# Shifts of the modulated norms: added per row tile with the eviction of plain transposes, in place of PSUM products with a selector and the identity

## The chip, the cores and the metric

The kernel runs on one core of one Trainium2 chip. The metric is device time in microseconds of one execution. Engines are named as the profile names them: PE (TensorE), ACT (ScalarE), DVE (VectorE), POOL (GpSimd), SP (SyncE, which issues the loads).

## The reference

Two blocks work on x [256, 1024] one after the other, all in float32. The first block (two layers) uses plain RMS norms. The second block modulates its norms by vectors made from a condition:

```python
def modulate(h, shift, scale):
    return h * (1 + scale[:, None, :]) + shift[:, None, :]

def macaron_ffn(x, mod3, norm_pre, norm_post, w_gate, w_up, w_down):
    h = modulate(rms_norm_2(x, norm_pre), mod3[:, 0], mod3[:, 1])
    y = (jax.nn.silu(h @ w_gate) * (h @ w_up)) @ w_down
    return x + MACARON_WEIGHT * mod3[:, 2][:, None, :] * rms_norm_2(y, norm_post)
...
        x = macaron_ffn(x, mod[:, 0:3], *ffn1)
        ctx = macaron_ffn(ctx, mod_ctx[:, 0:3], *ffn1)
...
            h_ctx_f, h_ctx_b = context_states(ctx, mod_ctx[:, 3:6], mix_norm_pre[layer], w_in[layer],
...
        x, _, _ = mix_sublayer(x, mod[:, 3:6], h_ctx_f, h_ctx_b, *mix)
        x = macaron_ffn(x, mod[:, 6:9], *ffn2)
```

`ctx` is a second sequence of 256 tokens. So the second block norms x three times and ctx twice with a scale and a shift per column, and each result is the input of a product with weights.

## The kernel before, in words

Tokens stand on the partitions in tiles of 128 (x has two, the context two). Products need the normed input the other way round, with the 1024 columns on partitions: eight row tiles of 128 columns by 128 tokens. Since float32 products are slow, every operand is held as two float32r parts whose sum is exact, a high part `hi` and a low part `lo`; a product is then three products. Weights are loaded by SP into one of three `raw` buffers, ACT writes their high part (L505) and DVE the low part (L506). The products are L519 (weights stationary, `mm_feat`) and L527 (activations stationary, `mm_tok`).

A norm (`pre_norm`, L545) works on one token tile: ACT squares it (L535), POOL makes the reciprocal root (L540, L542), and for each half of 512 columns DVE multiplies with that and with a gain row (L554, tile `xn`), PE turns the half into one bank of PSUM (tile `tp`, two buffers), and `split_to` takes it out: ACT writes `hi` (L510), then DVE writes `lo = tp - hi` (L511), each in one instruction of 128 x 512. Without a shift PE's part is four transposes (L559). With a shift, each of the four row tiles is a block of two products into one place of PSUM: the shift, held as 16 rows (two exact parts of eight row tiles), times a column of a selector (L561, float32r), and `xn` times the identity added to it (L563, float32, which runs as two passes, so two records each). `mod_gain` (L1171) makes the gain row and these 16 shift rows: ACT L1179, DVE L1181 and L1182, a transpose L1184, ACT L1186.

The norms with a shift are ten token tiles, that is 20 halves or 80 blocks, in four stages: the context's first norm (`context_norm`, L1049, beside the last products of the first block), x's first norm (`to_both`, L1059, between the first products for the context and the same products for x), the four tiles at the end of the joint feed-forward part (`ffn_both`, L1257 to L1267, with the gate and residual L1260 and L1264 before each norm, and units of the modulation, `ada`, L1131 to L1140, between), and the norm before the last feed-forward part (`boundary`, L1080). The boundaries of the first block have the same steps with plain transposes.

The order of the work on each engine is not the program's. `Order` (L207) collects all instructions, gives each a cost, and runs a list schedule: a step goes to the engine that can start first, and of the instructions that it could start then, to the first in the program. Tiles of one tag (`xn` has four, `tp` two, `raw` three) are handed out in program order. The result is pinned, so each engine runs its instructions in that order and a waiting one holds up all behind it. Its dependencies hold a bank of PSUM as one whole, and two accesses of it depend on each other even if both read:

```python
            whole = self.tags[t][0] == 'psum'
            for c, d, mm, k, kw in seen.get(t, ()):
                if (w or kw or whole) and c < b and a < d and m & mm:
                    need.add(k)
```

`finish` in `mix2` (L1553) already takes transposes out per row tile with a scalar per partition: ACT L1576 for `hi`, DVE L1577 for `lo`, each 128 x 128.

Of the kernel before, what the change touches and what calls it, by code (L numbers as in the profile page):

```python
# [10 lines left out]
FT = mybir.dt.float32  # L11
# [7 lines left out]
T = 256  # L19
# [13 lines left out]
def _tiles(w):  # L33
    """[1024, 128 n] -> [128, n, 8 * 128]: per output tile, the row tiles side by side."""
    n = w.shape[1] // 128
    return w.reshape(8, 128, n, 128).transpose(1, 2, 0, 3).reshape(128, n, 1024)
# [8 lines left out]
def _rows(w, n):  # L45
    """[128 k, c] -> [k / n, 128, n c]: n row tiles side by side."""
# [5 lines left out]
def _block_diag(w):  # L52
    """[4, 64, 64] -> [128, 2, 128]"""
# [7 lines left out]
def _ffn_up(a, b):  # L61
    """two [1024, 2816] -> [22, 128, 2048]"""
# [11 lines left out]
def shape_constants():  # L74
# [15 lines left out]
    # means over windows less the token itself: columns of tokens 0..143 from tokens 0..127, the rest from 128..255  # L90
# [113 lines left out]
# the units of the modulation that VectorE computes  # L204
# [3 lines left out]
class Order:  # L208
    """The order in which every engine issues the traced instructions: a list schedule with the engines' costs
    (Tile's own estimates are far off for float32 products and for GpSimd), pinned by issue-only edges.  # L210
    A step goes to the engine that can start first; among the instructions that it could start then, the one
    that comes first in the program goes."""
# [7 lines left out]
    # the clock of the tensor engine halves after a window that it was idle in for long  # L220
# [10 lines left out]
    # ---- what an instruction touches: (tile, partitions, columns as a bit mask); a bank of PSUM is one whole  # L231
# [19 lines left out]
    def graph(self):  # L251
        """dependencies: for each instruction the earlier ones it has to wait for"""
# [23 lines left out]
    # ---- costs  # L276
    def cost(self, i, e):
        """how long an instruction holds its engine; on the tensor engine also how long it streams"""
# [25 lines left out]
    # ---- the schedule  # L304
    def prepare(self):
# [8 lines left out]
        # activations of one table stay together  # L314
# [10 lines left out]
    def schedule(self, phases):  # L325
# [6 lines left out]
        # tiles: those of a tag are allocated in program order; a pool's once the pool before is done  # L332
# [103 lines left out]
class Pool:  # L436
    """a tile pool whose tiles the order knows"""
# [9 lines left out]
class Core:  # L447
# [33 lines left out]
    def outputs(self):  # L481
        """accumulators of a [256, 1024] product: per token tile, two banks of 512 columns"""
        self.o = [[self.acc_tile() for _ in range(2)] for _ in range(2)]
# [1190 lines left out]
```

## Time and profile before

| | us |
|---|---|
| runs shown, median (lowest to highest) | 1512.03 (1502.82 to 1514.5) |
| span of the profiled execution | 1506.0 |
| PE busy | 1466.4 |
| DVE busy | 905.6 |
| ACT busy | 683.5 |
| POOL busy | 78.5 |

The span runs from the first to the last instruction of the profiled execution, and the page gives no other time of it: 1506.0 lies inside the spread of the runs, 6.0 under their median. Busy PE includes time in which its matmuls are pipelined. In the rows below "A:B" is a stretch in us from the span's start, "x4" the number of instructions that a row merges, and "[1.20 <-DVE xn L554]" says that the engine sat idle for 1.20 us just before and what ended it. PEclk is the granted clock of PE as a share of 2.4 GHz.

### The profile page before, as it was taken

The page shows a single profiled execution, that of the slowest core. Times are in us where ns is not written, and L with a number is a line of the kernel's source. Part 1 is how long each engine was busy: PE and PEld are TensorE (multiplying, and loading weights), DVE is VectorE, ACT ScalarE, POOL GpSimd, SP SyncE. Part 2 cuts the span into 40 slices and gives each one's busy share as a digit, 9 for nine tenths or more (in the row PEclk, how much of TensorE's full clock was granted, in tenths as well). Part 3 has the DMA queues.
Part 4 walks back from the last instruction along what each step waited for, and adds up shares of the span by engine and source line. Part 5 has one row for each costly group of instructions (what it writes and reads, how often), then busy time and mean ns, then how long its engine had stood idle before and what let it go on. Part 6 is the DMA issues. An engine that isn't in the chain of part 4 may idle for free.

```text
span 1506.0 us, 21907 instructions
## 1 busy us (share of the span) xinstructions
PE 1466.4 (97%) x8857; PEld 1262.4 (84%) x8857; DVE 905.6 (60%) x1487; ACT 683.5 (45%) x1180; POOL 78.5 (5%) x146
## 2 busy tenths in 40 slices
PE   8999999999999999999999999999999998899998
PEld 7966999998877999988888888888697776699997
DVE  5667777777777777763774532454566536455554
ACT  5335655555345555552422222443544464454443
POOL 1002000002001000000000000000200212100000
PEclk8889999999789999998999999999999999799999
DMA  6407645546416554522555442232352033145552
GB/s 249 171 36 286 238 168 196 196 162 244 165 57 248 186 194 170 196 84 81 202 193 212 179 140 84 73 110 98 139 183 80 28 135 118 57 168 179 203 179 82
DMA packets 35833, 232.30 MB, mean 154 GB/s; under 512 B 4242, under 2 KB 5394, under 8 KB 10004
## 3 DMA queue, kind: packets, MB, share of 16 engines
q1 hardware_dynamic: 35732, 230.91, 42.6%
q8 instruction: 69, 1.13, 0.3%
q14 instruction: 32, 0.26, 0.0%
HBM read 229.85 MB, written 1.05 MB: 153 GB/s over the span
## 4 chain that ended last, share of the span: by engine, by line
PE 89%; DVE 3%; DMA 3%; ACT 2%; issue 1%; POOL 1%; SPq 0%; DVEq 0%; POOLq 0%; ACTq 0%
PE mm L519 39%; PE acc L527 25%; PE acc L519 11%; PE tp L563 3%; PE tp L561 1%; PE mm L839 1%; DVE wl L506 1%; PE mm L1131 1%; PE tp L856 1%; DMA raw<-in_fu_dram 1%; ACT wh L505 1%; PE tp L1167 1%; PE tp L711 1%; DMA raw<-in_wo_dram 0%; PE acc L1512 0%
## 5 line engine op out<-in xcount | busy, mean ns | idle before, releaser
L506 DVE TENSOR_TENSOR wl<-raw,wh 128x1024 fp32r<-128x1024 f32 (+2 forms) x345 | 414.0, 1209 | 281.9 <-ACT wh L505 270.3
L505 ACT ACTIVATE wh<-raw 128x1024 fp32r<-128x1024 f32 (+2 forms) x345 | 356.5, 1046 | 346.0 <-PE mm L519 178.1
L519 PE MATMUL mm<-hh,wh 128*128 128x256 f32 (+1 forms) x1440 | 228.0, 301 | 1.2 <-DVE ex L994 1.2
L519 PE MATMUL mm<-hl,wh 128*128 128x256 f32 (+1 forms) x1440 | 227.4, 298 | 0.0
L519 PE MATMUL mm<-hh,wl 128*128 128x256 f32 (+1 forms) x1440 | 223.0, 297 | 0.0
L519 PEld LDWEIGHTS mm<-hh,wh 128*128 128x128 f32 x1440 | 202.7, 195 | 11.6 <-ACT ex L992 1.4
L519 PEld LDWEIGHTS mm<-hl,wh 128*128 128x128 f32 x1440 | 202.0, 193 | 9.4
L519 PEld LDWEIGHTS mm<-hh,wl 128*128 128x128 f32 x1440 | 197.4, 193 | 6.6
L527 PE MATMUL acc<-wh,hl 128*128 128x512 f32 (+1 forms) x448 | 147.5, 393 | 0.7 <-DVE hl L511 0.4
L527 PE MATMUL acc<-wh,mid 128*128 128x512 f32 x352 | 114.1, 396 | 0.0
L527 PEld LDWEIGHTS acc<-wh,hl 128*128 128x128 f32 x448 | 84.8, 190 | 18.3 <-DVE hl L511 0.9
L527 PE MATMUL acc<-wh,midA 128*128 128x512 f32 (+1 forms) x304 | 92.3, 390 | 2.0 <-ACT wh L505 1.4
L994 DVE SCALAR_TENSOR_TENSOR ex<-mm,vec,ex 128x255 f32<-128x255 f32 (+1 forms) x176 | 84.3, 479 | 14.3 <-ACT ex L992 11.4
L527 PEld LDWEIGHTS acc<-wh,mid 128*128 128x128 f32 x352 | 63.6, 188 | 11.4
L540 POOL TENSOR_SCALAR ms<-msq 128x1 f32<-128x1 f32 x34 | 14.7, 432 | 1066.9 <-ACT junk L535 694.1
L527 PE MATMUL acc<-wl,mid 128*128 128x512 f32 x176 | 68.8, 392 | 0.0
L527 PE MATMUL acc<-wl,hl 128*128 128x512 f32 x176 | 68.6, 390 | 0.0
L527 PEld LDWEIGHTS acc<-wh,midA 128*128 128x128 f32 x304 | 55.5, 191 | 11.6 <-ACT wh L505 1.6
L992 ACT ACTIVATE ex<-mm,vec 128x256 f32<-128x256 f32 x88 | 48.9, 555 | 31.8 <-DVE ex L994 31.8
L527 PE MATMUL acc<-wl,midA 128*128 128x512 f32 (+1 forms) x152 | 56.1, 384 | 0.0
L892 DVE SCALAR_TENSOR_TENSOR ycv<-ga,vec,ycv 128x256 f32<-128x256 f32 x120 | 53.2, 478 | 0.8
L563 PE MATMUL tp<-eye,xn 128*128 128x128 f32 x160 | 44.5, 372 | 3.7 <-DVE xn L554 3.7
(341 smaller groups left out, 1881.6 us busy)
## 6 DMA issues: line engine op xcount, KB each, us to landing
raw<-in_fu_dram SPq DMA_DIRECT2D x44, 1024.0 KB, 4.9
raw<-in_ada_dram SPq DMA_DIRECT2D x22, 1024.0 KB, 4.9
raw<-in_fd_dram SPq DMA_DIRECT2D x22, 1024.0 KB, 4.8
raw<-in_f1u_dram SPq DMA_DIRECT2D x22, 1024.0 KB, 4.9
raw<-in_f2u_dram SPq DMA_DIRECT2D x22, 1024.0 KB, 4.9
raw<-in_wi_dram SPq DMA_DIRECT2D x20, 1024.0 KB, 5.2
raw<-in_adav_dram SPq DMA_DIRECT2D x14, 1024.0 KB, 5.1
raw<-in_wo_dram SPq DMA_DIRECT2D x12, 1024.0 KB, 6.9
```

Source lines behind the costliest of these rows:

```text
L505: self.nc.scalar.activation(hi[:, :n], raw, AF.Copy)
L506: self.nc.vector.tensor_sub(lo[:, :n], raw, hi[:, :n])
L519: self.nc.tensor.matmul(p, ww[:, k, :], hh[:, k, cols], start=n == 0, stop=n == 23)
L527: self.nc.tensor.matmul(p, aa, ww[:, s], start=first and n == 0, stop=last and n == 2)
L561: nc.tensor.matmul(p[:, k, :], shift, self.sel16[:, 4 * q + k:4 * q + k + 1].to_broadcast([16, 128]), start=True, stop=False)
L563: nc.tensor.matmul(p[:, k, :], xk, self.eye, start=False, stop=True)
L711: nc.tensor.matmul(p[:, :15], cw1[:, s, c, :], blk[s][:, c, :], start=c == 0, stop=c == 15)
L839: nc.tensor.matmul(s[:, j, :nk], qr[hd // 2][r, ts], ksl[j][r, :nk], start=True, stop=False)
L856: nc.tensor.matmul(o[:, c:c + 64], eT[:, j, b, :], vv[b][:, j * 64:(j + 1) * 64], start=b == 0, stop=b == t)
L892: nc.vector.scalar_tensor_tensor(ycv[i], ga[i][:, k:k + T], vcol('cw', 2 * k + i), ycv[i], op0=OP.mult, op1=OP.add)
L992: nc.scalar.activation(c[:, i, :], pg[:, i, :], AF.Identity, scale=col('fcw', 88 + m), bias=col('fcb', m))
L994: nc.vector.scalar_tensor_tensor(c[:, i, s:], pg[:, i, :T - s], col('fcw', 88 - 44 * s + m), c[:, i, s:], op0=OP.mult, op1=OP.add)
```

## The change

The products with the selector and the identity go. All norms use plain transposes; where there is a shift, the row tiles leave PSUM one by one, ACT adding the shift as a bias per partition, DVE adding it and subtracting `hi`. `mod_gain` hands on the shift column itself. The selector is no longer made.

```diff
         for q in range(2):
             s = slice(q * 512, (q + 1) * 512)
             xn = self.tmp([128, 512], 'xn', 4)
             nc.vector.scalar_tensor_tensor(xn, x[:, s], r, gain[:, s], op0=OP.mult, op1=OP.mult)
             p = self.tp_tile().rearrange('p (k t) -> p k t', k=4)
             for k in range(4):
-                xk = xn[:, k * 128:(k + 1) * 128]
-                if shift is None:
-                    nc.tensor.transpose(p[:, k, :], xk, self.eye)
-                    continue
-                nc.tensor.matmul(p[:, k, :], shift, self.sel16[:, 4 * q + k:4 * q + k + 1].to_broadcast([16, 128]),
-                                 start=True, stop=False)
-                nc.tensor.matmul(p[:, k, :], xk, self.eye, start=False, stop=True)
-            self.split_to(h[0][:, 4 * q:4 * q + 4, ts], h[1][:, 4 * q:4 * q + 4, ts], p)
+                nc.tensor.transpose(p[:, k, :], xn[:, k * 128:(k + 1) * 128], self.eye)
+            hi, lo = [m[:, 4 * q:4 * q + 4, ts] for m in h]
+            if shift is None:
+                self.split_to(hi, lo, p)
+                continue
+
+            for k in range(4):
+                b = shift[:, 4 * q + k:4 * q + k + 1]
+                nc.scalar.activation(hi[:, k, :], p[:, k, :], AF.Identity, bias=b)
+                nc.vector.scalar_tensor_tensor(lo[:, k, :], p[:, k, :], b, hi[:, k, :].bitcast(FT), op0=OP.add, op1=OP.subtract)
...
-        self.sel16 = self.const([16, KT], 'sel16', FR)
-        nc.vector.tensor_add(self.sel16, self.eye[:16, :8], self.eye[:16, 8:16])
...
     def mod_gain(self, i, pre, which):
         c = self.tmp([128, KT], 'gcol', 4)
         self.nc.vector.scalar_tensor_tensor(c, self.mod[:, 8 * i + 8:8 * i + 16, which], 1.0, self.v2[:, pre:pre + 8],
                                             op0=OP.add, op1=OP.mult)
-        nc = self.nc
-        sh = self.mod[:, 8 * i:8 * i + 8, which]
-        hi = self.tmp([128, KT], 'shi', 2, FR)
-        nc.scalar.activation(hi, sh, AF.Copy)
-        s2 = self.tmp([128, 2, KT], 'sh2', 2)
-        nc.vector.tensor_copy(s2[:, 0, :], hi.bitcast(FT))
-        nc.vector.tensor_sub(s2[:, 1, :], sh, hi.bitcast(FT))
-        p = self.tp_tile()[:16, :128]
-        nc.tensor.transpose(p, s2.rearrange('p a k -> p (a k)'), self.eye)
-        rows = self.tmp([16, 128], 'shr', 2, FR)
-        nc.scalar.activation(rows, p, AF.Copy)
-        return self.rows_of(c), rows
+        return self.rows_of(c), self.mod[:, 8 * i:8 * i + 8, which]
```

The rest of the diff takes out comments and docstrings.

## Rows read from the trace of the kernel before

**Rows 1.** The page's chain that ended last: shares by engine, then by line.

```profile
PE 89%; DVE 3%; DMA 3%; ACT 2%; issue 1%; POOL 1%; SPq 0%; DVEq 0%; POOLq 0%; ACTq 0%
PE mm L519 39%; PE acc L527 25%; PE acc L519 11%; PE tp L563 3%; PE tp L561 1%; PE mm L839 1%; DVE wl L506 1%; PE mm L1131 1%; PE tp L856 1%; DMA raw<-in_fu_dram 1%; ACT wh L505 1%; PE tp L1167 1%; PE tp L711 1%; DMA raw<-in_wo_dram 0%; PE acc L1512 0%
```

**Rows 2.** The four stages: length, busy PE, PEld, DVE, ACT, POOL; PEclk, DMA, GB/s.

```profile
657.00:671.00 14.00, 14.00 (x65) 10.12 (x64) 7.78 (x14) 4.09 (x10) 0.00 (x0) 1.00 0.01 1
...
691.40:708.70 17.30, 17.30 (x59) 12.82 (x58) 3.10 (x7) 3.42 (x5) 0.00 (x0) 0.61 0.07 13
...
1063.60:1081.20 17.60, 16.75 (x119) 9.90 (x119) 10.07 (x21) 8.19 (x18) 2.27 (x6) 1.00 0.69 252
1081.20:1099.80 18.60, 18.38 (x113) 15.11 (x113) 12.40 (x18) 10.83 (x20) 3.92 (x5) 1.00 0.21 76
...
1287.30:1310.50 23.20, 18.18 (x63) 13.04 (x61) 10.91 (x14) 8.57 (x20) 3.85 (x6) 0.61 0.27 91
```

**Rows 3.** Timeline: blocks of a shifted norm, early and late (start us, us).

```profile
668.82 0.32 PE L561 MATMUL tp<-sel,shr 16*128 16x128 f32 x1
...
669.07 0.49 PE L563 MATMUL tp<-eye,xn 128*128 128x128 f32 x2
...
669.49 0.32 PE L561 MATMUL tp<-sel,shr 16*128 16x128 f32 x1
...
1295.53 0.47 PE L561 MATMUL tp<-sel,shr 16*128 16x128 f32 x1
...
1296.66 0.47 PE L561 MATMUL tp<-sel,shr 16*128 16x128 f32 x1
```

**Rows 4.** Timeline: plain transposes of a boundary in the first block.

```profile
470.44 0.82 PE L559 MATMUL tp<-eye,xn 128*128 128x128 f32 x6
...
476.89 1.94 PE L559 MATMUL tp<-eye,xn 128*128 128x128 f32 x8 [3.27 <-DVE xn L554]
```

**Rows 5.** By line: evictions (ns min/median/max; L1477: busy us, mean ns).

```profile
L510 ACT ACTIVATE hh<-tp x36: 262/597/601, 10.7 to 1310.0; 128x512 fp32r<-128x512 f32 x28, 128x128 fp32r<-128x128 f32 x8
...
L511 DVE TENSOR_TENSOR hl<-tp,hh x36: 270/690/692, 11.3 to 1310.6; 128x512 fp32r<-128x512 f32 x28, 128x128 fp32r<-128x128 f32 x8
...
L1477 ACT ACTIVATE midA<-tp,gs 128x128 f32<-128x128 f32 x12 | 4.2, 373 | 0.0
...
L1577 DVE SCALAR_TENSOR_TENSOR midA<-tp,vec,midA x12: 341/345/351, 1251.0 to 1282.8; 128x128 fp32r<-128x128 f32 x12
```

**Rows 6.** Timeline of ACT in `finish`: one bank alone, then two banks.

```profile
1277.77 0.37 ACT L1576 ACTIVATE midA<-tp,vec 128x128 fp32r<-128x128 f32 x1 [0.63 <-PE tp L1571]
1278.70 0.37 ACT L1576 ACTIVATE midA<-tp,vec 128x128 fp32r<-128x128 f32 x1 [0.56 <-DVE midA L1577]
...
1251.27 0.63 ACT L1576 ACTIVATE midA<-tp,vec 128x128 fp32r<-128x128 f32 x2 [1.25 <-PE tp L1571]
1252.12 0.63 ACT L1576 ACTIVATE midA<-tp,vec 128x128 fp32r<-128x128 f32 x2 [0.22 <-DVE midA L1577]
```

**Rows 7.** The waits: who, for whom, us in total, times, longest.

```profile
DVE xn L573 <- ACT junk L535: 17.5, 13, 3.3
```

**Rows 8.** Timeline: last product for the context, last eviction of x's first norm.

```profile
690.40 1.12 PE L519 MATMUL acc<-hh,wl 128*128 128x256 f32 x8
...
707.06 0.60 ACT L510 ACTIVATE hh<-tp 128x512 fp32r<-128x512 f32 x1 [3.91 <-PE tp L563]
```

**Rows 9.** Timeline: the mixer's first product.

```profile
1081.21 0.72 PE L519 MATMUL mm<-midA,wh 128*128 128x256 f32 x4
```

**Rows 10.** Timeline: last product before, last eviction of a boundary, modulated then plain.

```profile
1286.96 0.40 PE L527 MATMUL acc<-wl,midA 128*128 128x512 f32 x1
...
1310.02 0.60 ACT L510 ACTIVATE hh<-tp 128x512 fp32r<-128x512 f32 x1 [3.21 <-PE tp L563]
...
467.56 0.39 PE L527 MATMUL acc<-wl,hh 128*128 128x512 f32 x1
...
478.87 0.60 ACT L510 ACTIVATE hh<-tp 128x512 fp32r<-128x512 f32 x1 [0.26 <-PE tp L559]
```

## The prediction

> **What bounds the kernel now.** I read first the page's chain that ended last, because busy shares alone don't say what a saving is worth. PE holds 89% of it, and among PE's lines stand the two that the change removes, L563 with 3% and L561 with 1% [rows 1]. Of a span of 1506.0 us that is about 60 us, so these products lie on the path, not beside it. Next I read the busy time by stage [rows 2]: A, the context's norm beside the last products of the first block (657 to 671); B, x's first norm (691.4 to 708.7); C, the four tiles at the end of the joint feed-forward part (1063.6 to 1099.8, two rows, cut where the mixer's first product starts [rows 9]); D, the boundary before the last part (1287.3 to 1310.5). In A and B PE has no gap, in C 1.1 us, in D 5.0 us. DVE and ACT are far from full in all of them, DVE at most 67%, in the second half of C. The timeline then gives the cost of a block: the next block starts 0.67 us later (668.82 to 669.49), and late in a stage 1.13 us later (1295.53 to 1296.66) [rows 3]. B and D have a granted clock of 0.61 on average [rows 2]: part of each runs at 2.4 GHz, part at 1.2.
>
> **What a block becomes on PE.** Six plain transposes took 0.82 us, eight after an idle stretch 1.94 us [rows 4]: 0.14 and 0.24 us each, ends included. So a block gives PE back 0.53 us at the high clock and 0.89 us at the low one. For 80 blocks that is 42 us if all ran fast, and about 50 us with some 22 of them (in B and D) slow.
>
> **What it becomes on ACT and DVE.** A half left PSUM with one ACT instruction of 0.60 us and one DVE instruction of 0.69 us [rows 5]. Now each half has four of each, 128 x 128. DVE's is the form of L1577, 0.345 us. ACT's, with a bias, is not in the trace with this function; the bare 128 x 128 copies of L510 start at 0.262, L1477, which has a bias per partition, takes 0.373 [rows 5], and I take 0.37. Busy time rises per half from 0.60 to 1.48 us on ACT and from 0.69 to 1.38 us on DVE.
>
> Busy time is not the whole price, because the two engines alternate. In `finish` ACT writes one row tile, and starts the next on the same bank only when DVE is done with the first: 1277.77 to 1278.70, 0.93 us for one row tile, 0.56 us of it idle for DVE [rows 6]. With two banks under way the pair of instructions starts at 1251.27 and again at 1252.12: 0.85 us for two row tiles [rows 6]. So a token tile (two halves, two `tp` buffers) takes 4 x 0.85 = 3.4 us if its halves overlap and 8 x 0.93 = 7.4 us if they don't. I take 3.4, since the list schedule starts whatever can start; 7.4 stays as the bound. That two reads wait for one another shows elsewhere too: L573 reads the accumulators that L535 reads, and waits 17.5 us for it in all [rows 7].
>
> The Trainium skill states this as a rule (PSUM — Partial Sum Buffer, section "PSUM bank collisions raise a hardware error ⚠️"): two engines must not touch one bank and quadrant at the same time, reads against reads included, and software has to keep them apart. By that rule the alternation stays whatever the order; without it eight ACT instructions of 0.37 us, 3.0 us in all, could run without DVE. Rows 6 and 7 agree with the rule, and it speaks against this change; what it does if the halves don't overlap is the slower rival below.
>
> What queues behind a waiting instruction: on ACT the squares L535 and the weight parts L505, on DVE the residuals (L577, L1264), L554 of the next tile and the weight parts L506; PE's next products wait for these, and SP's loads for the `raw` buffers that they free.
>
> **Stage by stage.**
>
> A: 16 blocks x 0.53 us = 8.5 us off PE, which has no gap there [rows 2]. The evictions, 2 x 3.4 us, have as cover the tail of the first block's products, which PE runs on with until the context's first product. I take 8. If the cover fails (2 x 7.4 us), half remains: bounds -4 and -8.5.
>
> B: the context's products end at 690.40 + 1.12 = 691.5, the last `hi` of x at 707.06 + 0.60 = 707.7 [rows 8]: 16.1 us. The transposes still come after those products, which stand earlier in the program. Then: half a tile of transposes 0.6, two banks out 3.4, four transposes at the low clock 1.0 once the first bank is free, two banks out 3.4: 8.4 us. Saved 7.7, I take 8. Now ACT and DVE are late, PE idles, and its clock stays low, as it is in rows 2 already. Bounds: banks one after the other (16 x 0.93 + 1.6 = 16.5), 0; transposes slipped between the context's products, -14.
>
> C: 32 x 0.53 = 17 us off PE. But DVE's busy time, 10.07 + 12.40 = 22.5 us [rows 2], grows by 8 x (1.38 - 0.69) = 5.5 to 28.0 us, and ACT's, 19.0, by 8 x 0.88 = 7.0 to 26.0. If this work stays in the stage, 36.2 us can't fall below 28.0: saved 8. The waits between the four tiles (squares, root, residual) then surface where PE's blocks covered them. Bounds: -1, where DVE's queue holds the residuals of the next tile back by half a tile's alternation (four tiles x 1.7 us, off the 8), and -17, where DVE's weight parts move behind the stage.
>
> D: from the last product to the last `hi` it is 1310.62 - 1287.36 = 23.3 us; the plain boundary of the first block takes 479.47 - 467.95 = 11.5 us [rows 10]. The difference, 11.8, is what blocks cost over transposes. Against it, the last tile's two evictions of 0.60 become 3.4 us (+2.2), and DVE has 1.4 us more before the second residual, of which half shows (+0.7). Saved 9. Bounds -4 (the last tile at 7.4 us) and -12.
>
> `mod_gain` loses five times one transpose, two ACT and two DVE instructions of 8 columns or 16 rows, and the selector is gone. They stand off the chain or in gaps; cover gone, they would be tenths of a microsecond each. I count nothing.
>
> **Sum:** -8 - 8 - 8 - 9 = -33 us, bounds -9 and -51. The profiled span, 1506.0, becomes 1473. The page gives no time of that execution beyond its span; the span lies within the runs shown and 6.0 under their median of 1512.0, on which I put the sum: 1479 us, 2.2% less.
>
> **Rivals.**
>
> 1. DVE and ACT become the bound more widely: splits of weights slip between the steps of the alternation, products start late, PE's clock stays low after the gaps. For it: DVE's 67% in C [rows 2], and one DVE queue for residuals and weights. Against it: PE's cover in A, and ACT and DVE under half busy in D. Half the gain: 1512 - 17 = 1495.
> 2. Everything hides: the transposes slip between products in B, weight parts move out of C. The lower bounds: 1512 - 51 = 1461. For it: the schedule may start `xn`'s transposes as soon as they are ready. Against: products earlier in the program go first.
> 3. Slower: the alternation on one bank, never overlapped, on the path everywhere. A row tile then takes 0.93 us [rows 6], 80 of them 74, and 20 halves lay 0.6 us of transposes ahead, 12: 86 us. Now the blocks and the last eviction of each tile cost about 60 + 10 x 1.3 = 73. That is +13: 1525. It decides from 0.76 us for each row tile on ((73 - 12) / 80; at the low clock's 1.13 a block it can't lose). Against it: 0.43 us with two banks [rows 6].
> 4. The new order, made from other costs over all instructions after the first `mod_gain`, loses elsewhere what is won here: 1510. Nothing in the rows speaks for it, but nothing excludes it.
>
> **How the numbers follow.** The forecast gets 0.55, the rivals 0.22, 0.13, 0.07 and 0.03. About 1%, 15 us, is what a measurement of this kernel can tell from no change. The forecast, rival 2 and some 0.13 of rival 1 are faster by more: 0.81; the rest of rival 1 and rival 4 make 0.12; rival 3 makes 0.07. The range goes from 1456 (rival 2 with 5 us of other order) to 1500 (rival 1 with the same), leaving out rivals 3 and 4 and some edges.
>
> **What would show it.** Right: no L561; 80 transposes in place of 160 records with about 0.14 us each; 80 ACT and 80 DVE instructions of 128 x 128 at about 0.37 and 0.345 us, pairs 0.85 us apart; D from its last product to its last `hi` about 14 us, B about 8, C about 28 with DVE nearly full. Wrong: row tiles 0.9 us apart throughout, a stage C as long as now with PE idle for DVE, or stages that shrink while the rest of the span grows.

## The result, and the profile after

The changed kernel took 1468.01 us in the median of 4 runs (1464.97 to 1479.94), the kernel before, beside it on the same chip, 1511.41 us (4 runs, 1502.82 to 1514.5). The ratio is 0.9707, 95% interval 0.9663 to 0.9751: 2.9% faster, some 43 us. The forecast was 1479 us. The profiled execution has a span of 1478.1 us and a time of 1479.94 us, so 1.8 us lie around the span; it was the longest of its four runs. Over all runs of this study 1.8 to 2.3 us do.

The page of the changed kernel: span, busy times, and the chain that ended last, by engine and by line.

```profile
span 1478.1 us, 21683 instructions
...
PE 1428.5 (97%) x8692; PEld 1236.1 (84%) x8692; DVE 913.5 (62%) x1536; ACT 695.1 (47%) x1230; POOL 78.5 (5%) x146
...
PE 89%; DVE 3%; DMA 3%; ACT 2%; issue 1%; POOL 1%; SPq 0%; DVEq 0%; POOLq 0%; ACTq 0%
PE mm L519 40%; PE acc L527 26%; PE acc L519 11%; PE mm L839 1%; PE mm L1131 1%; PE tp L557 1%; PE tp L856 1%; DVE wl L506 1%; ACT wh L505 1%; DMA raw<-in_fu_dram 1%; PE tp L1167 1%; PE tp L1464 1%; ACT junk L535 1%; PE tp L711 1%; DMA raw<-in_wo_dram 1%
```

The chain's shares by engine are those of [rows 1] to the percent; what went is L563 with 3% and L561 with 1%, and the plain transposes L557 hold 1%. PE is still the chain.

The changed evictions by line (ns min/median/max; first and last start), ACT's first, then DVE's, then the transposes on PE (144, of them 80 of shifted norms).

```profile
L565 ACT ACTIVATE hh<-tp,mod x48: 348/367/392, 655.9 to 1282.2; 128x128 fp32r<-128x128 f32 x48
L565 ACT ACTIVATE midA<-tp,mod x32: 349/367/398, 1047.6 to 1075.9; 128x128 fp32r<-128x128 f32 x32
...
L566 DVE SCALAR_TENSOR_TENSOR hl<-tp,mod,hh x48: 338/343/352, 656.7 to 1282.6; 128x128 fp32r<-128x128 f32 x48
...
L557 PE MATMUL tp<-eye,xn x144: 270/273/476, 9.3 to 1279.4; 128*128 128x128 f32 x144
```

0.367 and 0.343 us stand where the prediction took 0.37 and 0.345 from [rows 5]. The transposes are 80 as counted.

The stages by window, in the columns of [rows 2]: A with the context's products, B, C in two parts (to the last `hi`, then to the first eviction of the token-major products), D.

```profile
654.80:680.20 25.40, 25.40 (x172) 23.09 (x171) 20.31 (x41) 15.53 (x42) 4.18 (x8) 1.00 0.01 2
680.20:688.40 8.20, 5.25 (x32) 4.55 (x31) 5.46 (x20) 5.50 (x16) 0.00 (x0) 0.85 0.83 332
1042.70:1076.30 33.60, 28.08 (x212) 22.31 (x212) 28.48 (x69) 26.09 (x66) 5.45 (x10) 0.85 0.45 173
1076.30:1091.10 14.80, 14.80 (x89) 14.76 (x88) 10.37 (x16) 7.41 (x11) 0.00 (x0) 1.00 0.63 220
1267.30:1282.70 15.40, 6.89 (x33) 5.11 (x32) 13.08 (x27) 11.20 (x31) 4.18 (x6) 0.69 0.32 104
```

For comparison every stage is cut at the same events in all kernels. A: first transposing instruction of the context's norm to the end of the context's products. B: from there to the last `hi` of x. C: first product of the modulation (L1131) to the first eviction of the mixer's token-major products. D: last L527 to the last `hi`. "Rest" is the span less these four. All of it is read from the timelines of the profiled executions, in us (the first row is the profile of before that the prediction used):

```
kernel             A      B      C      D     sum    rest    span
before           34.40  16.14  56.53  23.26  130.3  1375.7  1506.0
before, again e6 34.40  14.83  66.33  23.32  138.9  1382.7  1521.6
after            25.42   8.11  48.45  15.20   97.2  1380.9  1478.1
after, again e1  25.42   8.11  47.90  15.19   96.6  1362.7  1459.3
after, again e12 25.42   8.11  47.96  15.21   96.7  1366.0  1462.7
e2 no shift      25.47   3.75  45.22  14.10   88.5  1370.3  1458.8
e3 narrow, old   34.38  18.70  61.76  25.43  140.3  1375.0  1515.3
e4 hi first      25.45   6.93  49.95  13.64   96.0  1369.3  1465.3
e5 wide add      25.46  14.27  52.79  18.67  111.2  1374.9  1486.1
e7 ACT adds      25.43  11.81  50.33  16.77  104.3  1372.1  1476.4
e8 identity      27.28   9.06  50.47  17.49  104.3  1371.1  1475.4
e9 wide in place 25.45   5.07  51.33  16.35   98.2  1371.0  1469.2
e10 ACT in place 25.46   6.94  48.55  15.75   96.7  1366.6  1463.3
e11 f32 selector 42.99  21.18  80.60  26.31  171.1  1372.9  1544.0
```

From the first row to the third the four stages give 9.0, 8.0, 8.1 and 8.1 us: 33.2 in all. The rest, in which both kernels do the same work but for the few small instructions of `mod_gain`, is 5 us longer in this one execution. So the span fell by 27.9 us, less than the medians did; why these two differ is the subject of e1, e6 and e12.

### The profile page after: what moved, and what is told of

Read it like the earlier page. It is cut to its first block, busy times and chain, and to the rows that moved or that the text cites. A ratio compares the mean times of both kernels' runs of the same rounds, so it can differ in the third digit from the quotient of the medians.

```text
span 1478.1 us, 21683 instructions
## 1 busy us (share of the span) xinstructions
PE 1428.5 (97%) x8692; PEld 1236.1 (84%) x8692; DVE 913.5 (62%) x1536; ACT 695.1 (47%) x1230; POOL 78.5 (5%) x146
## 4 chain that ended last, share of the span: by engine, by line
PE 89%; DVE 3%; DMA 3%; ACT 2%; issue 1%; POOL 1%; SPq 0%; DVEq 0%; POOLq 0%; ACTq 0%
PE mm L519 40%; PE acc L527 26%; PE acc L519 11%; PE mm L839 1%; PE mm L1131 1%; PE tp L557 1%; PE tp L856 1%; DVE wl L506 1%; ACT wh L505 1%; DMA raw<-in_fu_dram 1%; PE tp L1167 1%; PE tp L1464 1%; ACT junk L535 1%; PE tp L711 1%; DMA raw<-in_wo_dram 1%
## 5 line engine op out<-in xcount | busy, mean ns | idle before, releaser
L527 PE MATMUL acc<-wh,hl 128*128 128x512 f32 (+1 forms) x448 | 147.3, 392 | 1.1 <-DVE hl L511 0.4
L527 PE MATMUL acc<-wh,mid 128*128 128x512 f32 x352 | 113.6, 395 | 0.0
L527 PEld LDWEIGHTS acc<-wh,hl 128*128 128x128 f32 x448 | 84.7, 189 | 18.8 <-DVE hl L511 0.9
L527 PE MATMUL acc<-wh,midA 128*128 128x512 f32 (+1 forms) x304 | 91.3, 390 | 3.3 <-ACT wh L505 2.8
L994 DVE SCALAR_TENSOR_TENSOR ex<-mm,vec,ex 128x255 f32<-128x255 f32 (+1 forms) x176 | 84.3, 479 | 14.3 <-ACT ex L992 11.4
L527 PEld LDWEIGHTS acc<-wh,mid 128*128 128x128 f32 x352 | 63.4, 188 | 11.2
L527 PE MATMUL acc<-wl,mid 128*128 128x512 f32 x176 | 68.8, 392 | 0.0
L527 PE MATMUL acc<-wl,hl 128*128 128x512 f32 x176 | 68.5, 389 | 0.0
L527 PEld LDWEIGHTS acc<-wh,midA 128*128 128x128 f32 x304 | 55.8, 192 | 12.3 <-ACT wh L505 3.0
L527 PE MATMUL acc<-wl,midA 128*128 128x512 f32 (+1 forms) x152 | 56.8, 393 | 0.0
L1154 DVE SCALAR_TENSOR_TENSOR gg<-raw,ee 128x1024 bf16<-128x1024 f32 x40 | 46.9, 1220 | 3.2 <-ACT ee L1168 3.2
```

Of the source, the lines that this page charges most:

```text
L527: self.nc.tensor.matmul(p, aa, ww[:, s], start=first and n == 0, stop=last and n == 2)
L994: nc.vector.scalar_tensor_tensor(c[:, i, s:], pg[:, i, :T - s], col('fcw', 88 - 44 * s + m), c[:, i, s:], op0=OP.mult, op1=OP.add)
L1154: nc.vector.scalar_tensor_tensor(junk, w[:, q * D:(q + 1) * D], 1.0, self.srow[c], op0=OP.mult, op1=OP.mult, accum_out=m[:, q, c:c + 1])
```

## The experiments

**e1 and e12: the changed kernel again; e6: the kernel before again.** No edit. They ask how far a profile of one execution stands for the kernel.

> The changed kernel once more, for a second profile of it. Its first profile ends 28 us before that of the kernel before, its times 43 us. By stage the first profile is 37 us ahead when the eight-column-group products of the mixer begin and loses some 9 us from there to the last boundary, at a granted clock of 0.82 to 0.87 where the kernel before had 0.96 to 1.00. Theory: that loss belongs to the execution, not to the change; a second profile shows the stages A to D at the same lengths within 1 us (A 9, B 8, C 8, D 8 us shorter than before) and the mixer at another length. Rival: the loss belongs to the change (its order or its shorter activity), and the mixer is again about 9 us longer than before the change. Time 1465 to 1480 us by both.

> The changed kernel on the same chip, to compare e9_add_in_place and e10_act_in_place with: 1462 to 1478 us, A 25.4, B 8.1, D 15.2 us once more; C by its clock 47.9 to 48.5.

> The kernel before once more, for a second profile of it: stages A 34.4, B 16.1, C 56.5, D 23.3 us again within 1 us, whatever the span. Theory: what two profiles differ in outside these stages is the granted clock of single stretches in the first block and the mixer. Rival: stage lengths move from one execution to the next as much as the 8 us that the change takes from each.

Measured: e1 1464.51 us (4 runs; before 1512.36, 13 runs), ratio 0.965 (0.9613 to 0.9686). e12 1467.34 us (6 runs; before 1514.73, 11 runs), 0.9707 (0.9663 to 0.975). e6 1523.41 us, one run. In the table A, B and D come out alike to 0.1 us in the three profiles of the changed kernel, C to 0.6. The rest does not: 1380.9, 1362.7, 1366.0. The mixer shows where. The stretch from C's end to D, cut at the same three events, in the changed kernel's first profile:

```profile
1091.10:1148.30 57.20, 57.20 (x300) 45.98 (x299) 38.95 (x84) 26.31 (x43) 4.48 (x10) 1.00 0.36 124
1148.30:1177.80 29.50, 27.13 (x91) 19.27 (x89) 12.73 (x17) 11.71 (x24) 5.77 (x8) 0.77 0.00 1
1177.80:1267.40 89.60, 82.06 (x458) 64.93 (x457) 43.57 (x83) 46.25 (x110) 15.54 (x24) 0.90 0.28 106
```

and in e1, the same program:

```profile
1083.10:1140.30 57.20, 57.20 (x299) 45.96 (x299) 39.06 (x85) 26.28 (x43) 4.47 (x10) 1.00 0.36 124
1140.30:1165.40 25.10, 22.75 (x90) 16.54 (x89) 12.65 (x17) 11.56 (x24) 5.76 (x8) 0.93 0.00 1
1165.40:1248.40 83.00, 76.64 (x458) 60.05 (x457) 43.31 (x83) 46.07 (x110) 15.79 (x24) 0.98 0.31 115
```

The instruction counts agree within one, the busy time of DVE and ACT within 0.3 us a row, and ahead of the second row PE was busy for all of 57.20 us at 1.00 in both. Yet the second row has a granted clock of 0.77 against 0.93 and the third 0.90 against 0.98: 11.0 us between two executions of one program. The same can fall into a stage. C of the kernel before in e6:

```profile
1067.10:1084.80 17.70, 16.86 (x115) 9.91 (x115) 10.07 (x21) 8.19 (x18) 2.37 (x6) 0.94 0.68 251
1084.80:1103.00 18.20, 18.20 (x65) 14.99 (x64) 7.79 (x11) 7.83 (x14) 3.82 (x5) 0.50 0.13 45
1103.00:1133.40 30.40, 30.40 (x185) 28.63 (x185) 18.73 (x29) 13.45 (x21) 0.00 (x0) 0.94 0.36 126
```

In the first profile of that kernel C ran at 1.00 from end to end. Here the granted clock is 0.50, the lower level, in the second row, in which many blocks stand, and C is 9.8 us longer. In e3, which has the same products, C is 61.8 us at 0.92. So the profile that the prediction was built on showed C at its better, and e6's rival holds for C: the 8.1 us that the change takes from it are the difference of two executions, and against e6 they would be 17.9.

Over all runs of the study: 35 of the kernel before have a mean granted clock of 0.9586 (0.951 to 0.970), 14 of the changed one 0.9664 (0.957 to 0.972). A line through the times against the mean clock, with one slope for all kernels of the study (12.7 us for 0.01) and a height for each, leaves a scatter of 1.2 us. On it the two kernels differ by 36 us at one mean clock; the other 10 us or so of their means (1513.5 and 1467.8) go with the higher clock. Part of that belongs to the stages themselves (B at 0.61 and 0.85), and these runs don't separate it from chance.

**e2: the shift left out.** It prices all that the narrow evictions cost.

```diff
-            for k in range(4):
-                b = shift[:, 4 * q + k:4 * q + k + 1]
-                nc.scalar.activation(hi[:, k, :], p[:, k, :], AF.Identity, bias=b)
-                nc.vector.scalar_tensor_tensor(lo[:, k, :], p[:, k, :], b, hi[:, k, :].bitcast(FT), op0=OP.add, op1=OP.subtract)
+            self.split_to(hi, lo, p)
```

> Plain transposes as in the change, but each half leaves PSUM with one ACT and one DVE instruction of 128 x 512, and the shift is not added at all (left out of the computation). It takes the eviction's price out of the change. Theory: the alternation of ACT and DVE shows in B and D and partly in C; without it the last high part of stage B comes about 4 us after the context's products instead of 8.2, that of D about 12 us after the last product instead of 15.2, C some 3 us earlier; together 8 to 12 us under the changed kernel. Rival: the narrow evictions are hidden, PE's time was the whole price; within 3 us of the changed kernel.

Measured 1457.63 us (4 runs), ratio 0.961 (0.9568 to 0.9652); the changed kernel on the same chip (e1) 1464.51. The stages are 8.1 us shorter than e1's: B 4.4, C 2.7, D 1.1, A nothing. So the narrow evictions as a whole, their alternation and their longer busy time together, cost about 8 us in the stages, 7 in the medians and 3 on the line above. It lies in B above all, where nothing stands beside it; in A, where the first block's products run on, it is hidden, as the prediction said.

**e4: the order inside a half.** All four of ACT's instructions come first in the program, then DVE's four.

```diff
             for k in range(4):
-                b = shift[:, 4 * q + k:4 * q + k + 1]
-                nc.scalar.activation(hi[:, k, :], p[:, k, :], AF.Identity, bias=b)
-                nc.vector.scalar_tensor_tensor(lo[:, k, :], p[:, k, :], b, hi[:, k, :].bitcast(FT), op0=OP.add, op1=OP.subtract)
+                nc.scalar.activation(hi[:, k, :], p[:, k, :], AF.Identity, bias=shift[:, 4 * q + k:4 * q + k + 1])
+            for k in range(4):
+                nc.vector.scalar_tensor_tensor(lo[:, k, :], p[:, k, :], shift[:, 4 * q + k:4 * q + k + 1],
+                                               hi[:, k, :].bitcast(FT), op0=OP.add, op1=OP.subtract)
```

> The changed kernel with the order inside a half turned: the four ACT instructions first, then the four DVE ones. Same instructions. Theory: two reads of one bank wait for one another, so in the old order four pairs alternate; in groups a half takes 4 x 0.26 us on ACT and then as much on DVE, the high parts of a tile are ready about 1 us earlier, and B and D each shorten by 1 to 2 us: 2 to 5 us faster than the changed kernel. Rival: the order inside a half makes no difference (the two halves overlap anyway): within 1.5 us.

Measured 1465.55 us (1459.91 to 1472.84), 0.9664 (0.9616 to 0.9711): no gain over e1. B and D are 1.2 and 1.6 us shorter, but C is 2.0 longer: PE's idle time in it is that of e1 (5.6 and 5.8 us), but PE is busy for 44.4 us in place of 42.1, at a granted clock of 0.90 in place of 0.93. The alternation can be shortened where it stands alone; what lengthens C here isn't shown.

**e3: narrow evictions with the old products.** Relative to the kernel before: blocks stay, but each row tile leaves by itself.

```diff
-            self.split_to(h[0][:, 4 * q:4 * q + 4, ts], h[1][:, 4 * q:4 * q + 4, ts], p)
+            hi, lo = [m[:, 4 * q:4 * q + 4, ts] for m in h]
+            if shift is None:
+                self.split_to(hi, lo, p)
+                continue
+            for k in range(4):
+                self.split_to(hi[:, k, :], lo[:, k, :], p[:, k, :])
```

> The kernel before with its products of selector and identity, but each half leaves PSUM per row tile: four ACT copies and four DVE subtractions of 128 x 128 in turn. The change's evictions without its transposes. Theory: with PE spending 0.67 or 1.13 us on a row tile, the alternation (0.43 to 0.93 us for a row tile) lies almost wholly beside PE; only the last half of each stage stands on the path, 4 x 2 to 3 us, so 5 to 12 us slower than the kernel before. Rival, the slower case of the prediction: the alternation doesn't overlap and costs about 0.9 us for each of 80 row tiles on the path; 20 us slower or more.

Measured 1512.88 us (10 runs, 1500.49 to 1521.54), ratio 0.9991 (0.9955 to 1.0027). The expected loss is not there. B and D are 2.6 and 2.2 us longer than before's first profile, A the same; C (61.8) lies between the two profiles of before. Whether those 5 us are real and made good elsewhere, or lie within what one profile differs from the next, this run doesn't say; on the line above e3 and the kernel before differ by 0.3 us. It does say that narrow evictions are cheap beside blocks, and that the gain is the blocks'. They are a little cheaper here than the change's: without the shift a row tile takes 0.28 us on ACT and 0.29 on DVE, in place of 0.37 and 0.34.

**e8: the identity product alone.** The shift leaves as in the change, but the transpose of a shifted norm is a float32 product with the identity, as it was.

```diff
-                nc.tensor.transpose(p[:, k, :], xn[:, k * 128:(k + 1) * 128], self.eye)
+                xk = xn[:, k * 128:(k + 1) * 128]
+                if shift is None:
+                    nc.tensor.transpose(p[:, k, :], xk, self.eye)
+                else:
+                    nc.tensor.matmul(p[:, k, :], xk, self.eye, start=True, stop=True)
```

> The changed kernel with the identity product (float32, two passes) in place of the plain transpose in the modulated norms; the selector product stays out. PE pays about 0.42 us for a row tile instead of 0.14, or 0.72 instead of 0.24 at the low clock. Theory: PE's time on these row tiles lies on the path where PE has no gap; A grows by 16 x 0.28 = 4.5 us, C by up to 9, B and D by 2 to 4 each, where the alternation already takes 0.43 us for a row tile: 10 to 20 us slower than the changed kernel. Rival: the evictions are the bound now and hide a slower PE; within 4 us of it.

**e11: the selector product in float32.** Relative to the kernel before: `sel16` and the shift's rows in float32, as the identity and `xn` are.

```diff
-        self.sel16 = self.const([16, KT], 'sel16', FR)
+        self.sel16 = self.const([16, KT], 'sel16')
...
-        rows = self.tmp([16, 128], 'shr', 2, FR)
+        rows = self.tmp([16, 128], 'shr', 2)
```

> The kernel before with its selector product in float32 instead of float32r (the 16 shift rows and the selector as float32 tiles, nothing else). In e8_identity_product two passes of the identity product without a selector product between them took about 0.24 us for a row tile, where they take 0.42 of a block's 0.67 beside the selector product. Theory: what makes a block dear is the change between the two kinds of product within it; with one kind a block is four passes of about 0.12, so 0.45 to 0.50 us instead of 0.67, and A shortens by 3 us, the whole by 8 to 15 us against the kernel before. Rival: the selector product itself is dear whatever its kind, and in float32 it has two passes: a block takes 0.67 us or more, and the time is that of the kernel before or more.

Measured: e8 1470.48 us (4 runs, 1468.99 to 1477.66), 0.9733 (0.9685 to 0.9781), 2 to 6 us over the change's three medians where 10 to 20 were expected. e11 1545.16 us (1542.62 to 1554.24), 1.0222 (1.0176 to 1.0268): slower than the kernel before, by 30 us in the medians (1514.73 beside it).

The three kinds of row tile stand at the head of A, at a granted clock of 1.00 until then. The changed kernel, four plain transposes and the next product:

```profile
654.80 0.60 PE L557 MATMUL tp<-eye,xn 128*128 128x128 f32 x4
655.16 0.71 PE L527 MATMUL acc<-wh,mid 128*128 128x512 f32 x2
```

e8, four row tiles as identity products (L561 there):

```profile
655.89 1.06 PE L561 MATMUL tp<-eye,xn 128*128 128x128 f32 x8
656.70 0.72 PE L527 MATMUL acc<-wh,mid 128*128 128x512 f32 x2
```

e11, a block with the selector in float32:

```profile
653.06 0.48 PE L561 MATMUL tp<-sel,shr 16*128 16x128 f32 x2
653.48 0.49 PE L563 MATMUL tp<-eye,xn 128*128 128x128 f32 x2
653.90 0.48 PE L561 MATMUL tp<-sel,shr 16*128 16x128 f32 x2
```

From start to start, a row tile holds PE 0.36 / 4 = 0.09 us as a plain transpose, 0.81 / 4 = 0.20 as an identity product (two records each: x8 for four row tiles), 0.67 as a block [rows 3], and 0.84 as a block in float32, whose selector product too now has two records. So of the 0.58 us that a block lost, some 0.11 is the identity product against the transpose, and 0.47 goes with the selector product between. A bears this out: e8's A is 27.28 - 25.42 = 1.9 us longer than the change's, 0.12 for each of its 16 row tiles. I had suspected that a block is dear because PE changes between float32r and float32 inside it; with one type throughout, e11 should then have been cheaper. It was dearer by 0.17 us a block, and that theory fell. What it took beyond 80 x 0.17 = 14 us went with the clock: the mean granted clock of its runs is 0.937 to 0.944, and its C is 80.6 us at 0.70.

The trace of the kernel before narrows it further. In A some of its blocks are cut apart by products of the first block (L527, float32r, 128 rows):

```profile
660.02 0.32 PE L561 MATMUL tp<-sel,shr 16*128 16x128 f32 x1
660.27 0.51 PE L527 MATMUL acc<-wh,mid 128*128 128x512 f32 x1
...
661.32 0.39 PE L527 MATMUL acc<-wl,mid 128*128 128x512 f32 x1
661.54 0.40 PE L527 MATMUL acc<-wh,mid 128*128 128x512 f32 x1
661.77 0.38 PE L563 MATMUL tp<-eye,xn 128*128 128x128 f32 x2
```

What follows a selector product starts 0.25 us after it, the identity product into the same place of PSUM (668.82 to 669.07 [rows 3]) and L527 into another bank alike (660.02 to 660.27). The identity product behind an L527 starts after 0.23 us, much as an L527 does there (0.22). So here neither the change of type nor the shared place costs anything that shows; the cost stands beside the selector product. Whether its 16 rows make it, or its one column spread over 128, wasn't tried apart.

e8 fell short of its expected price on PE first: a row tile pays 0.11 us more, not the 0.28 expected, and A grew by 1.9 us, not 4.5. Its stages are 7.7 us longer than e1's. Its time shows less than that, and its runs have the highest clocks of the study on the mean, 0.970 to 0.976; at one mean clock it lies 12.5 us over the change by the line through the runs (under e1). In its B the granted clock is 1.00, in the change's 0.85, though PE is idle there nearly as long (2.5 us of 9.1, against 3.0 of 8.2). What makes that difference these runs don't show.

**e5, e7, e9, e10: other ways to add the shift.** All add it in one step from PSUM into SBUF, and split there in one wide instruction per engine, without alternation. In e5 DVE adds over four row tiles at once, in e7 ACT adds row tile by row tile; both take a further `xn` tile from the ring of four. e9 and e10 are the same two with the sum written back over `xn`.

```diff
+            v = self.tmp([128, 512], 'xn', 4).rearrange('p (k t) -> p k t', k=4)
+            nc.vector.tensor_tensor(v, p, shift[:, 4 * q:4 * q + 4, None].to_broadcast([128, 4, 128]), op=OP.add)
+            self.split_to(hi, lo, v)
```

(e5, in place of the change's loop; e9 has `v = xn.rearrange('p (k t) -> p k t', k=4)` as its first line. e7 and e10 have these first lines, and in place of the second:)

```diff
+            for k in range(4):
+                nc.scalar.activation(v[:, k, :], p[:, k, :], AF.Identity, bias=shift[:, 4 * q + k:4 * q + k + 1])
```

> The changed kernel, but DVE adds the shift to a half in one instruction of 128 x 512 as it leaves PSUM (into an xn tile, the shift broadcast along the tokens), and the two parts are made from that tile in one instruction each. ACT and DVE no longer alternate on a bank; ACT's busy time for a half falls from 1.48 to 0.60 us, DVE's stays (two instructions of 0.69 instead of four of 0.345). Theory: the alternation is what is left of the price; B shortens from 8.1 to about 6.5 us, D from 15.2 to about 14, C (to the end of the token-major products, 48 us) by 0 to 3 since DVE stays as busy and the xn ring is used more: 3 to 6 us faster than the changed kernel. Rival: DVE's busy time is the bound, so nothing is gained; within 2 us of it, or slower where the ring of four xn tiles holds back the residuals.

> The changed kernel, but ACT alone empties a bank: four instructions with the shift as bias into an xn tile, one after the other, then both parts from that tile in one instruction each (ACT 128 x 512, DVE 128 x 512). ACT's busy time for a half becomes about 4 x 0.26 to 0.37 + 0.62, 1.7 to 2.1 us, DVE's 0.69 instead of 1.38. Theory: the alternation goes, a tile takes about 3.6 us on ACT alone: B and D about as long as in the changed kernel (within 1.5 us), C where DVE was nearly full shortens by 1 to 3 us: between 0 and 4 us faster. Rival: ACT becomes the bound in C, 2 to 6 us slower.

> As e5_add_wide (DVE adds the shift to a half in one instruction of 128 x 512, both parts from the sum in one instruction each), but the sum goes back into the xn tile that the half came from, so that no tile of the ring is taken more than in the changed kernel. Theory: what made e5_add_wide slower was the ring of four xn tiles, which holds back the next tile's residual and norm; with it out of the way B takes about 6.5 us, D about 14, C (to the end of the token-major products) 45 to 48, and the time is 2 to 6 us under the changed kernel. Rival: the longer chain of a half (add, high part, low part of 128 x 512 each) is what costs; B 11 us or more again, and the time 10 us or more over the changed kernel.

> As e7_act_adds (ACT alone empties a bank with four biased instructions, both parts from that tile in one instruction each), but back into the half's own xn tile. Theory (the ring was at fault): B about 8 us instead of 11.8, D about 15, and the time within 4 us of the changed kernel. Rival (ACT's chain is at fault): B and D as in e7_act_adds, 11.8 and 16.8 us.

Measured: e5 1484.61 us (6 runs), 0.982 (0.9779 to 0.9861); e7 1478.57 us (4), 0.9753 (0.9688 to 0.9819); e9 1471.72 us (6), 0.9736 (0.9702 to 0.9771); e10 1471.59 us (4), 0.9729 (0.9683 to 0.9775). The change has 0.965 to 0.9707 in its three measurements, so none is faster: e5 is slower by over 1%, e7 stands between, and e9 and e10, on one chip with e12, are some 4 us over it, which their intervals don't tell from nothing. On the line through the runs the four lie 12.5, 5.3, 2.4 and 1.8 us over the change. Why e5 is slow, DVE's timeline in its B shows:

```profile
688.95 0.75 DVE L554 SCALAR_TENSOR_TENSOR xn<-x,rs,grow 128x512 f32<-128x512 f32 x1 [1.89 <-POOL rs L542]
690.97 0.69 DVE L564 TENSOR_TENSOR xn<-tp,mod 128x512 f32<-128x512 f32 x1 [1.27 <-PE tp L557]
691.58 0.74 DVE L554 SCALAR_TENSOR_TENSOR xn<-x,rs,grow 128x512 f32<-128x512 f32 x1
```

and that of e9, the same stretch:

```profile
672.40 1.42 DVE L554 SCALAR_TENSOR_TENSOR xn<-x,rs,grow 128x512 f32<-128x512 f32 x2 [1.89 <-POOL rs L542]
674.44 1.29 DVE L564 TENSOR_TENSOR xn<-tp,mod 128x512 f32<-128x512 f32 x2 [0.62 <-PE tp L557]
```

In e5 the tile's second `xn` comes 2.63 us after the first, behind the first half's sum (L564); in e9 the two stand together, and B is 5.1 instead of 14.3 us. The ring of four, now shared with the sums, held the second half back; e10 has a B of 6.9 us where e7, which takes from the ring too, has 11.8. e9's B is also 3.0 us shorter than the change's: without alternation B does get faster. It loses this in C (51.3 against 48.0) and D (16.4 against 15.2), where two weight parts stand ahead of the last tile's `xn` on DVE, in e9's D:

```profile
1267.82 2.35 DVE L506 TENSOR_TENSOR wl<-raw,wh 128x1024 fp32r<-128x1024 f32 x2
1271.01 1.41 DVE L554 SCALAR_TENSOR_TENSOR xn<-x,rs,grow 128x512 f32<-128x512 f32 x2 [0.84 <-POOL rs L542]
```

How much of D's 1.1 us these two account for wasn't tried apart.

## Why the prediction was right

The time lies in the range and 11 us under the forecast, and the direction and the mechanism are those that were forecast. Its steps:

**A, forecast -8, measured -9.0.** PE has no gap there before and after, so all that a row tile gives back counts: 16 x (0.67 - 0.09) = 9.3. The term was a little mis-sized in the transpose: 0.14 us came from [rows 4] with the last one's end included; from start to start it is 0.09. So the bound of -8.5 was passed.

**B, forecast -8 to 8.4 us, measured -8.0 to 8.1 us.** The forecast named each piece; here they are. ACT in B of the changed kernel:

```profile
680.70 3.17 ACT L565 ACTIVATE hh<-tp,mod 128x128 fp32r<-128x128 f32 x8 [2.87 <-PE tp L557]
684.56 0.37 ACT L565 ACTIVATE hh<-tp,mod 128x128 fp32r<-128x128 f32 x1 [0.69 <-PE tp L557]
685.34 0.62 ACT L565 ACTIVATE hh<-tp,mod 128x128 fp32r<-128x128 f32 x2 [0.42 <-DVE hl L566]
686.13 0.63 ACT L565 ACTIVATE hh<-tp,mod 128x128 fp32r<-128x128 f32 x2 [0.16 <-DVE hl L566]
686.91 0.63 ACT L565 ACTIVATE hh<-tp,mod 128x128 fp32r<-128x128 f32 x2 [0.16 <-DVE hl L566]
687.96 0.37 ACT L565 ACTIVATE hh<-tp,mod 128x128 fp32r<-128x128 f32 x1 [0.42 <-DVE hl L566]
```

and PE, the two groups of transposes:

```profile
680.06 1.04 PE L557 MATMUL tp<-eye,xn 128*128 128x128 f32 x8
683.86 1.10 PE L557 MATMUL tp<-eye,xn 128*128 128x128 f32 x8 [2.76 <-DVE hl L566]
```

The pairs start 0.79 us apart (685.34, 686.13, 686.91), where the banks of `finish` gave 0.85 [rows 6]. The two halves overlap, a tile takes ACT 3.2 and 3.8 us, and the second tile's transposes wait 2.76 us for L566, until the first tile has left its banks. The prediction weighed a rule of the Trainium skill (PSUM — Partial Sum Buffer, section "PSUM bank collisions raise a hardware error ⚠️"), by which software has to keep two engines apart on one bank, reads included. The trace shows it kept: the second tile's transposes are all done at 684.96, and still ACT waits for L566 ahead of every pair after that. It is the kernel's own order that makes it wait; what happens when two engines do read one bank at once, no run here shows. That the alternation stays "whatever the order" was too strong: in e4's B ACT's eight instructions of the first tile take 2.17 us in one stretch, not 3.17, with most of DVE's behind them. e2 and e4 put the price on it: some 8 us in the stages for narrow evictions as a whole, 1.2 of B's 8.1 for the order within a half. One thing of the forecast was off: PE's clock in B is 0.85 on average, not the lower level.

**C, forecast -8, measured -8.1.** The busy times were sized well: to the last `hi` DVE is busy for 28.48 us where 28.0 was forecast, ACT for 26.09 where 26.0 was. But this part takes 33.6 us, not 28: DVE isn't full, and of the forecast 8 us only 2.6 are saved here (36.2 before). The other 5.5 come behind the last `hi`. C of the kernel before as a whole, and its part behind the last `hi`:

```profile
1063.60:1120.10 56.50, 55.44 (x362) 45.31 (x362) 36.50 (x60) 29.25 (x53) 6.18 (x10) 1.00 0.45 160
1099.80:1120.10 20.30, 20.30 (x134) 20.30 (x133) 14.03 (x21) 10.23 (x15) 0.00 (x0) 1.00 0.46 158
```

Products of the mixer had moved ahead into PE's gaps between the tiles, so that 14.8 us are left behind the last `hi` where 20.3 were. PE's busy time in C fell from 55.4 to 28.08 + 14.80 = 42.9 us, 12.6 less, and its idle time rose from 1.1 to 5.5; the difference, within the rounding of the windows, is the 8.1. So the number was right and the reason half right, and that it came out to a tenth is luck. What limits the first part is not DVE's busy time but waits from step to step, and PE at a granted clock of 0.85, where the kernel before had 1.00 in its first profile (in e6 0.50 in part of the stage). The two weren't tried apart; e1's C, at 0.93 as a whole where the changed kernel's first profile has 0.89, is 0.6 us shorter.

**D, forecast -9 to 14 us, measured -8.1 to 15.2 us.** It came out close, but two terms behind it were further off and nearly made each other good, which is luck. The forecast took the plain boundary of the first block, 11.5 us, as the base and put 2.9 us of narrow evictions on it. e2 has plain transposes and wide evictions in D itself, and its D is 14.1 us: the base was 2.6 us too short. Most of that lies ahead of the first tile. Its `xn` starts 0.7 us after the last product's end in the plain boundary (467.56 + 0.39 [rows 10] to 468.68) and 2.4 us after it in D (1266.99 + 0.40 to 1269.77); first the plain boundary in the kernel before, then D in the changed one:

```profile
468.68 1.42 DVE L554 SCALAR_TENSOR_TENSOR xn<-x,rs,grow 128x512 f32<-128x512 f32 x2
```

```profile
1266.99 0.40 PE L527 MATMUL acc<-wl,midA 128*128 128x512 f32 x1
1269.77 1.42 DVE L554 SCALAR_TENSOR_TENSOR xn<-x,rs,grow 128x512 f32<-128x512 f32 x2 [0.86 <-POOL rs L542]
```

The narrow evictions cost 15.2 - 14.1 = 1.1 us, not 2.9. The last tile in D, on PE and on ACT:

```profile
1277.79 2.03 PE L557 MATMUL tp<-eye,xn 128*128 128x128 f32 x8 [5.89 <-DVE hl L566]
```

```profile
1278.94 0.37 ACT L565 ACTIVATE hh<-tp,mod 128x128 fp32r<-128x128 f32 x1 [2.14 <-PE tp L557]
...
1282.22 0.37 ACT L565 ACTIVATE hh<-tp,mod 128x128 fp32r<-128x128 f32 x1 [0.16 <-DVE hl L566]
```

From the first of its transposes to the last `hi` it is 1282.59 - 1277.79 = 4.8 us, of which the alternation from its first to its last instruction takes 3.65. In e2 it is 2.6, so the 2.2 us that were forecast for the last tile are there. But its transposes start 10.4 us after the last product, in e2 11.5: the order of the work ahead of it gave half of them back.

**`mod_gain`, forecast nothing.** No stage shows a trace of it, and the rest shows nothing that exceeds what one program differs by.

**The sum and where it was put.** The four terms were -8, -8, -8, -9; the profile of that same execution against the first of the changed kernel gives -9.0, -8.0, -8.1, -8.1, 33.2 for 33. So close a sum owes something to luck, in C and D above all. The step that failed is the last one: the sum was made in one execution and set on the median, as if every execution had those stages. The medians differ by 10 us more. Two things that the profiles show can lie in it, and their shares stay open: C of the kernel before is 56.5 us in one profile and 66.3 in another, as part of its blocks ran at the lower clock; and the rest of the span runs from 1363 to 1383 us over fourteen profiles of kernels that do the same in it, with 1369.9 as the mean of three for the change and 1379.2 of two for the kernel before. The profile used was also a quicker execution of its kernel: 1506.0 + 1.8 = 1507.8 us by the time around the span that the other runs show, 3.6 under the median. The first profile of the changed kernel is of a long one, 11.9 us over its own median. That is why the spans fell by 27.9 us only.

**The rivals.** Rival 1 (1495): in C's first part products do start late, PE is idle for 5.5 us there, and weight parts do slip in (e9's D), but half the gain didn't go. Something like it happens in e5, for another reason. Rival 2 (1461): all three medians of the change (1464.5 to 1468.0) are nearer to its time than to the forecast's 1479, but its mechanism isn't there; B's transposes did not slip between products, and the stages gave 33 us, not 51. Rival 3 (1525): the pitch that decides is 0.76 us for each row tile; measured are 0.79 for two. Rival 4 (1510): the rest of the span is 5 us longer in the first profile, which is less than one program differs from itself, and on the means it is shorter.

None of the versions tried that add the shift beats the change.

## What to carry to other kernels

A product that only moves or spreads data costs PE its passes and what stands between them; here the small selector product, with what it holds up beside it, was the dearer part of a block, so adding the term on the way out of PSUM was worth it even though eight instructions take the place of two. Price the alternation of two engines on one bank by its pair pitch with two banks, not by busy time. Take the base of a stage from that stage and not from one like it elsewhere: D's was 2.6 us longer. See also that new temporaries don't come out of a ring that the next step needs. Set a sum of stages on a median only after a second profile: where a stage runs at either clock level, one execution can hide a quarter of a gain.

## What was not expected of the hardware

Two executions of one program gave the mixer's stretch 176.3 and 165.3 us with the same instruction counts and busy times of DVE and ACT, at granted clocks of 0.91 and 0.98 over it; and C of the kernel before ran once at 1.00 and once, through some of its blocks, at 0.50, with PE busy throughout (18.20 of 18.20 us) in the slower case. What decides between them is not shown by these runs.

A float32 identity product holds PE 0.20 us a row tile by itself, but a block of it with a selector product of 16 rows takes 0.67, more than three times as much. With both in float32 it is 0.84. At a granted clock of 1.00 what follows the float32r selector product starts 0.25 us after it, in float32 into the same place or in float32r into another bank, while the same identity product behind a product of 128 rows of the other type starts as any other does.
